# Bias rows written in the first phase, split weights of the output projection kept in DRAM, masks with buffers of their own

## The chip, the core and the metric

The kernel runs on one core of a Trainium2 chip. The metric is device time in microseconds (us) of one execution; lower is better. Engines are named as the profile names them: PE (TensorE matmuls), PEld (its weight loads), DVE (VectorE), ACT (ScalarE), POOL (GpSimd) and SP (SyncE, which here issues every DMA from one queue).

## The reference

One layer for 1024 tokens of width 2048, cut to what matters here:

```python
z = rms_norm(h, norm_g) @ w_in                    # one projection for all branches
o_rw = rwkv7_mixer(z_rw, ...)                     # 16 recurrent heads of 64
# sparse attention, 16 heads, per block of 128 queries:
score = einsum('bqh,bqhs->bqs', wi, relu(einsum('bqhd,bsd->bqhs', qi, k_idx)))
score = where(admissible, score, -inf)            # chunk-causal
_, sel = top_k(score, 256)                        # 256 keys per query
logits = einsum('bqhr,bqkr->bqhk', qa, kv_sel) + bias_tab[t5_bucket(sel - q_pos)]
o_ds = softmax(where(valid, logits, -inf)) @ kv_sel @ w_uv
h = h + concat([o_rw * silu(g_rw), o_ds * silu(g_ds)]) @ w_out
h = h + (p @ w_ple) * sigmoid(h @ w_pg)
out = rms_norm(h, final_g)
```

## The kernel before, in words

Matmuls with weights run on operands split in two fp32r parts (`wh` and `wl`, made by `w_piece`: one 256 KB load, a copy on ACT, a subtraction on POOL), three matmuls for each pair of tiles. A recording layer (`Sched`) takes every instruction with a level and writes out, at each `emit`, an order for all five engines by a list schedule with its own costs; so every instruction has the same line, L382, in the profile, and a small change moves many. An engine runs its instructions strictly in the order written.

The stages are these.

1. Projection and the recurrent branch, in 16 units (8 head pairs by two halves of 512 tokens). At its end PE is filled up with `wout_rw(0)`, the recurrent branch's half of the output projection for the first token half: 16 column tiles `n`, each with two weight pieces `w_o[n, 0]` and `w_o[n, 1]`, 24 matmuls `pz<-mh,wh` and so on. 13 tiles are recorded in this stage, three later.
2. Scoring: for 16 index heads and the query blocks `qt` 2 to 7, PE makes `pix`, ACT `rl` (Relu), DVE adds into the mask row `mk` of that block, `(qt + 1) * 128` wide. PE is filled up with the rest of `wout_rw(0)` and with `wout_rw(1)`, the second token half, which loads and splits the same 32 weight pieces again.
3. Search: the 256th largest score of each row is found bit by bit in 31 rounds, blocks 2 to 4 by counts on DVE (`jk`), blocks 5 to 7 by Sign with a sum on ACT (`js`); DVE turns the counts into the next threshold `th`. Evacuations of `wout_rw(1)` (`h<-pz,h` on DVE, with `h` loaded from `xt`) and the first attention operands stand among it.
4. Masks: `pick_keys(qt)` for `qt` 2 to 7 turns scores and threshold into 0 or -1e30, with two scratch rows `eq` and `gt`.
5. Attention, 8 head pairs `u` by 8 query blocks: `softmax` adds mask and bias (`mb` on POOL, then `lgt` on DVE), takes Exp on ACT; `weigh` transposes and multiplies by the values. Its score rows `lgt` use tag `L` of pool `at`, three buffers of 128x1024; `eq` and `gt` use the same three.
6. The rest of the output projection, the gate and the last norm, where PE sets the time.

The bias rows: 16 heads' bias by distance is a 16x384 table `vb`; `bsk` holds 128 copies of each row in DRAM, so that a skewed read gives a 128x256 tile `bt` for a head. Before the change the table is made between scoring and `wout_rw(1)`, and one DMA writes all 3 MB of `bsk` from SBUF.

The lines that the change and the steps below touch are in `wout_rw`, `pick_keys`, the block under `nc.level(LG)` that starts with `rb0`, and the attention loop over `u` and `qt`.

Of the kernel before, what the change touches and what calls it, by code (L numbers as in the profile page):

```python
# [15 lines left out]
OP = mybir.AluOpType  # L16
# [369 lines left out]
def hybrid_kernel(ctx, tc, cst, msk, bkt, prm, xt, pt_, w_z, w_z80, w_lora, w_uq, w_iq, w_uk, w_uv, w_o, w_pg,  # L386
# [6 lines left out]
    qnd, ckd = ([[dt(f"{n}{j}_{h}", [128, TH]) for h in range(2)] for j in range(m)] for n, m in (("qn", 3), ("ck", 2)))  # L393
    kid = [dt(f"ki{h}", [64, TH]) for h in range(2)]
    gdd, h1d = ([[dt(f"{n}{j}_{h}", [128, TH]) for h in range(2)] for j in range(m)] for n, m in (("gd", 8), ("h1", 16)))
    bsk = dt("bsk", [16, 128, 384])

    def pool(stack, keep=None, **kw):
        p_ = Pool(nc, stack.enter_context(tc.tile_pool(**kw)), kw["bufs"])
# [497 lines left out]
    def wout_in(hf):  # L897
# [9 lines left out]
                nc.gpsimd.tensor_tensor(ML[g][:, k, :], raw, MH[g][:, k, :], op=OP.subtract)  # L907
        return MH, ML

    def wout_rw(hf, MH, ML, tiles):  # L910
        for n in tiles:
            pz = gemm(lambda g: w_o[n, g], 128, 8, lambda k: MH[k // 4][:, k % 4, :], lambda k: ML[k // 4][:, k % 4, :])
            h_ = big_t("h1")
            nc.sync.dma_start(h_, xt[n * 128:n * 128 + 128, hf * TH:hf * TH + TH])
            with nc.level(LEVAC):
                nc.vector.tensor_tensor(h_, pz, h_, op=OP.add)
                store(h1d[n][hf], h_)

    units = [(u, hf) for hf in range(2) for u in range(8)]
    was, Z, RES, Y = {}, {}, {}, {}  # L920
# [24 lines left out]
    with nc.level(LG):  # L945
        Z[0], was[0] = first_unit(0)
        for n, (u, hf) in enumerate(units):
            sub(2 * n)
            if hf == 0:
                with nc.level(LF):  # L950
                    if u < 5:
                        gds(u, hf)
                    elif u == 5:
                        dsa_lat(0)
                if u == 7:
                    for j, pg in zip((5, 6, 7), zgroup((43, 44, 45))):
                        gds(j, 0, pg)
                    sub(2 * n + 1)
                    Z[n + 1], was[1] = first_unit(1)
                    continue  # L960
            elif u == 0:
                with nc.level(LF):
                    dsa_lat(1)
            if n < 15:
                Z[n + 1] = zunit(*units[n + 1])
            sub(2 * n + 1)
        sub(32)
        with nc.level(LF):
            for j in range(8):
                gds(j, 1)  # L970
            MW = wout_in(0)
            wout_rw(0, *MW, range(NWO))
# [67 lines left out]
                                 start=(j == 0), stop=(j == 1))  # L1040
        return pl[:, :Sn]

    def rb(a, i):
        return bass.AP(tensor=a.tensor, offset=a.offset + i * 16, ap=[[0, 32], [1, 16]])

    with nc.level(LX):
        for j in range(3):
            split_in([(0, h, qnd[j][h]) for h in range(2)], QH[:, j, :], QL[:, j, :], nc.vector)
# [25 lines left out]
                        nc.vector.scalar_tensor_tensor(MK[qt], r_, w_, MK[qt], op0=OP.mult, op1=OP.add)  # L1074

    with nc.level(LG):
        rb0 = sm.tile([32, 16], F32, name="rb0")
        nc.sync.dma_start(rb0, rel_bias)
        rb1 = sm.tile([32, 16], F32, name="rb1")
        nc.sync.dma_start(rb1, rb(rel_bias, 15))  # L1080
        nc.vector.tensor_tensor(rb0, rb0, rb1, op=OP.subtract)
        oh = at.tile([32, 384], F32, name="oh", tag="L")
        nc.sync.dma_start(oh, bkt)
        pvb = pg_tile()
        nc.tensor.matmul(pvb[:16, :384], rb0, oh, start=True, stop=True)
        vb = at.tile([16, 384], F32, name="vb", tag="L")
        nc.vector.tensor_copy(vb, pvb[:16, :384])
        nc.sync.dma_start(bsk, vb[:, None, :].to_broadcast([16, 128, 384]))
        MW1 = wout_in(1)
        with nc.level(LF):  # L1090
            wout_rw(0, *MW, range(NWO, 16))
        wout_rw(1, *MW1, range(16))
# [12 lines left out]
    def pick_keys(qt):  # L1105
        Sn = (qt + 1) * 128
        t_, n_ = KEYS[qt][:2]
        eq = at.tile([128, 1024], F32, name="eq", tag="L")[:, :Sn]
        nc.gpsimd.tensor_scalar(eq, MK[qt], t_, None, op0=OP.is_equal)
        gt = at.tile([128, 1024], F32, name="gt", tag="L")[:, :Sn]  # L1110
        nc.vector.tensor_scalar(gt, MK[qt], t_, None, op0=OP.is_gt, op1=OP.add, accum_out=n_)
        nc.vector.tensor_scalar(n_, n_, -1.0, 256.0, op0=OP.mult, op1=OP.add)
        nc.vector.tensor_tensor_scan(MK[qt], one.to_broadcast([128, Sn]), eq, 0.0, op0=OP.mult, op1=OP.add)
        nc.vector.scalar_tensor_tensor(eq, MK[qt], n_, eq, op0=OP.is_le, op1=OP.mult)
        (nc.vector if qt in FINV else nc.gpsimd).tensor_tensor(MK[qt], gt, eq, op=OP.add)
        nc.scalar.activation(MK[qt], MK[qt], AF.Copy, scale=BIG, bias=-BIG)

    def count(qts, sign=False, op=OP.is_ge):
# [13 lines left out]
    with nc.level(LX):  # L1132
        for qt in range(2, 8):
            Sn = (qt + 1) * 128
            nc.vector.memset(MK[qt][0:64, Sn - 64:Sn], NINF)

        for qts in (BY_COUNT, *BY_SIGN):
            th, xm, cn, pd = group(qts)  # L1140
            neg = 0x80000000 if qts in BY_SIGN else 0
            nc.vector.memset(th, 0)
            count(qts)
            nc.vector.tensor_scalar(xm, cn, 255.5, None, op0=OP.is_lt)
            nc.vector.memset(th, 0x40000000 | neg)
            nc.vector.memset(pd, 0xBFFFFFFF ^ neg)
            nc.vector.copy_predicated(th, xm, pd)
        for bit in range(30, -1, -1):
            for qts in (*BY_SIGN, BY_COUNT):
                th, xm, cn, pd = group(qts)  # L1150
                sign = qts in BY_SIGN
                count(qts, sign)
                for qt, x, n, few in ([(qt, *KEYS[qt][2:0:-1], 512.0 - 128 * (qt + 1) - 0.5) for qt in qts] if sign else
                                      [(0, xm, cn, 255.5)]):
                    nc.vector.tensor_scalar(x, n, few, float(1 << bit), op0=OP.is_lt, op1=OP.mult)
                nc.vector.scalar_tensor_tensor(th, xm, (1 << bit) >> 1, th, op0=OP.bitwise_or, op1=OP.bitwise_xor)
        for g, qts in enumerate(BY_SIGN):
            p_, _, cn, _ = group(qts)
            nxt = lambda n, dt: consts.tile([128, len(qts)], dt, name=f"{n}{g}")
            ts, tt = nc.vector.tensor_scalar, nc.vector.tensor_tensor  # L1160
            ts(p_, p_, 0x80000000, None, op0=OP.bitwise_xor)
            lo, hi, sg, up = (nxt(n, U32) for n in ("nlo", "nhi", "nsg", "nup"))
            d, c, b = (nxt(n, F32) for n in ("nd", "nc", "nb"))
            ts(lo, p_, 0xFFFF, None, op0=OP.bitwise_and)
# [12 lines left out]
            ts(sg, cn, 255.5, None, op0=OP.is_ge)
            nc.vector.copy_predicated(p_, sg, up)
        for qt in range(2):
            Sn = (qt + 1) * 128  # L1180
            nc.gpsimd.memset(MK[qt], 0.0)
            nc.gpsimd.memset(MK[qt][0:64, Sn - 64:Sn], -BIG)
        for qt in range(2, NFIN):
            pick_keys(qt)
    CH = xn.tile([128, 2, T], F32R, name="CH", tag="xh0")
    CL = xn.tile([128, 2, T], F32R, name="CL", tag="xl0")
# [124 lines left out]
    with nc.level(LG):  # L1311
# [191 lines left out]
```

## Time and profile before

| what | value |
|---|---|
| median of 3 runs | 2894.11 us (2889.0 to 2895.61) |
| the profiled execution's own time | 2892.14 us |
| its span, first to last instruction | 2890.4 us |
| granted TensorE clock, mean | 0.968 |
| PE busy | 2696.4 us (93%) |
| DVE, ACT, POOL busy | 1641.3, 1500.9, 1381.8 us |
| DMA | 268.15 MB, 93 GB/s over the span |

The profiled execution lies 2.0 us below the median and inside the runs' range. Busy shares are means over stages that have different limits; the stages are told apart by the strips of 40 slices (72 us each) and by windows.

### The profile page before, as it was taken

The numbers are of one execution on the slowest core, as the hardware profiler recorded it, in microseconds if no ns is written. First come the engines' busy times: TensorE is split into PE (matmuls) and PEld (weight loads), VectorE is DVE, ScalarE is ACT, GpSimd is POOL, SyncE is SP. The second block draws the span as 40 slices with busy tenths as digits, with TensorE's granted clock in tenths as the row PEclk, the third lists the DMA queues.
The fourth block names the chain that finished last, engine by engine and source line by source line (L and its number), as shares of the span: only waits on it lengthen the run. The fifth ranks groups of instructions, "written<-read, shape, count | busy, mean of one in ns | idle before, by whom it ended". The sixth has DMA issues, their size and how long they took to land. (4 is left out here: it accounts for less than half of the span.)

```text
span 2890.4 us, 46558 instructions
## 1 busy us (share of the span) xinstructions
PE 2696.4 (93%) x16482; PEld 2158.0 (75%) x16482; DVE 1641.3 (57%) x3709; ACT 1500.9 (52%) x3297; POOL 1381.8 (48%) x1403
## 2 busy tenths in 40 slices
PE   7999999999999999999999999726999999999997
PEld 6777877877787887887877778614776688878885
DVE  5566666446862566666665578777666551125312
ACT  4455555435653455555554566695677533333332
POOL 5544555554464555455445542113333355556564
PEclk9999999999999999999999999858999999999998
DMA  4222222222233222222224533511223243345332
GB/s 156 84 65 61 74 74 76 82 87 70 91 118 91 73 72 67 71 70 70 76 90 152 181 119 106 105 27 27 69 63 93 79 156 95 99 151 172 110 98 91
DMA packets 158489, 268.15 MB, mean 93 GB/s; under 512 B 21648, under 2 KB 43184, under 8 KB 158256
## 3 DMA queue, kind: packets, MB, share of 16 engines
q1 hardware_dynamic: 158256, 265.18, 30.1%
q8 instruction: 130, 2.13, 0.3%
q14 instruction: 103, 0.84, 0.1%
HBM read 221.33 MB, written 35.39 MB: 89 GB/s over the span
## 5 line engine op out<-in xcount | busy, mean ns | idle before, releaser
L382 POOL TENSOR_TENSOR wl<-wr,wh 128x512 fp32r<-128x512 f32 (+2 forms) x656 | 860.2, 1314 | 824.3 <-ACT wh L382 746.8
L382 ACT ACTIVATE wh<-wr 128x512 fp32r<-128x512 f32 (+2 forms) x656 | 403.8, 618 | 752.7 <-PE pz L382 567.5
L382 PE MATMUL pz<-xh,wh 128*128 128x512 f32 (+1 forms) x1504 | 610.1, 408 | 12.8 <-ACT wh L382 9.0
L382 PE MATMUL pz<-xh,wl 128*128 128x512 f32 (+1 forms) x1504 | 610.8, 408 | 1.5 <-POOL wl L382 1.3
L382 PE MATMUL pz<-xl,wh 128*128 128x512 f32 (+1 forms) x1504 | 608.4, 406 | 0.0
L382 PEld LDWEIGHTS pz<-xh,wh 128*128 128x128 f32 (+1 forms) x1504 | 286.1, 190 | 61.6 <-ACT wh L382 10.0
L382 PEld LDWEIGHTS pz<-xh,wl 128*128 128x128 f32 (+1 forms) x1504 | 285.0, 190 | 49.6 <-POOL wl L382 3.0
L382 PEld LDWEIGHTS pz<-xl,wh 128*128 128x128 f32 (+1 forms) x1504 | 285.8, 190 | 47.7 <-DVE xl L382 0.3
L382 DVE SCALAR_TENSOR_TENSOR tg<-tg,pg 128x512 f32<-128x512 f32 x32 | 22.0, 687 | 315.4 <-ACT tg L382 315.4
L382 PE MATMUL pz<-hh,wl 128*128 128x512 f32 x512 | 199.3, 389 | 0.0
L382 PE MATMUL pz<-hh,wh 128*128 128x512 f32 x512 | 199.3, 389 | 0.0
L382 PE MATMUL pz<-hl,wh 128*128 128x512 f32 x512 | 199.2, 389 | 0.0
L382 DVE CAST_PREDICATED QX<-MS,pq 128x512 f16<-128x512 uint8 x160 | 110.2, 689 | 146.9 <-PE pq L382 145.9
L382 POOL TENSOR_TENSOR mb<-mk,bt 128x256 f32<-128x256 f32 (+1 forms) x128 | 90.4, 710 | 161.4 <-DVE mx L382 136.5
L382 ACT ACTIVATE Ztb<-pzt 64x256 f16<-64x256 f32 x320 | 120.6, 377 | 62.4 <-PE pzt L382 57.0
L382 ACT ACTIVATE lgt<-lgt,nm 128x128 f32<-128x128 f32 (+7 forms) x128 | 98.9, 773 | 60.2 <-DVE nm L382 58.8
L382 PEld LDWEIGHTS pz<-hh,wh 128*128 128x128 f32 x512 | 96.1, 188 | 20.0
L382 PEld LDWEIGHTS pz<-hh,wl 128*128 128x128 f32 x512 | 96.1, 188 | 20.0
L382 PEld LDWEIGHTS pz<-hl,wh 128*128 128x128 f32 x512 | 96.1, 188 | 19.9
L382 ACT ACTIVATE js<-mk,th 128x1024 f16<-128x1024 f32 (+2 forms) x93 | 96.7, 1040 | 25.5 <-DVE xm L382 21.4
L382 ACT ACTIVATE Sw<-UV,Wx 64x64 f32<-64x64 f32 x240 | 82.2, 343 | 52.7 <-DVE UV L382 49.4
L382 PE MATMUL pz<-mh,wh 128*128 128x512 f32 x256 | 101.6, 402 | 3.0 <-ACT mh L382 2.3
(331 smaller groups left out, 5981.6 us busy)
## 6 DMA issues: line engine op xcount, KB each, us to landing
wr<-in_w_z_dram SPq DMA_DIRECT2D x368, 256.0 KB, 2.6
wr<-in_w_pg_dram SPq DMA_DIRECT2D x128, 256.0 KB, 2.5
wr<-in_w_o_dram SPq DMA_DIRECT2D x120, 256.0 KB, 2.7
h<-h SPq DMA_DIRECT2D x60, 256.0 KB, 2.7
h<-in_xt_dram SPq DMA_DIRECT2D x32, 256.0 KB, 3.1
out_dram<-h SPq DMA_DIRECT2D x32, 256.0 KB, 2.3
gd<-gd SPq DMA_DIRECT2D x16, 256.0 KB, 2.3
mix<-m SPq DMA_DIRECT2D x32, 128.0 KB, 1.7
```

What stands on the lines that cost most here:

```text
L382: getattr(self.real[o.eng], o.name)(*o.args, **o.kw)
```

## The change

Three edits, and what follows from them.

- **Bias rows.** The table is made in the first unit of stage 1 (`bias_table`), stored to DRAM (`vbd`), and each of the 16 units records one DMA from DRAM to DRAM that writes one head's 128 copies (`bias_copies`). The one DMA of 3 MB between scoring and search is gone, and `oh` and `vb` leave tag `L`.
- **Kept weight parts.** `wout_rw(0)` stores both parts of each of its 32 weight pieces to DRAM (64 stores of 256 KB); `wout_rw(1)` loads both parts (64 loads) instead of loading and splitting the piece again (32 loads, 32 ACT copies, 32 POOL subtractions).
- **Masks.** `gt` is written over the scores in `mk`. `eq` becomes fp16; for blocks 2 to 4 `eq` and the running count `up` use the count's own scratch tag `jk`, for blocks 5 to 7 `eq` uses tag `js` and `up` takes one buffer of tag `L`. Blocks 5, 6 and 7 are recorded inside the attention loop of the first head pair, each one step ahead of the step that needs it (ahead of steps 4, 5 and 6).

```diff
-POOLH, FINV = (), (2, 3, 4, 5, 6, 7)
-NMR, NFIN, FAHEAD, PIECES = 1, 8, 1, (0, 1, 2)
+POOLH = ()
+NMR, PIECES = 1, (0, 1, 2)
...
+    def kept(n, g):
+        if (n, g) in parts:
+            pair = []
+            for d, nm in zip(parts[n, g], ("wh", "wl")):
+                t = wp.tile([128, 4, 128], F32R, name=nm, tag=nm, bufs=W_[1])
+                nc.sync.dma_start(t.bitcast(F32), d)
+                pair.append(t)
+            return pair
+        pair = w_piece(w_o[n, g], 4, 128)
+        parts[n, g] = [dt(f"wo{n}_{g}{a}", [128, 4, 128]) for a in "hl"]
+        for d, t in zip(parts[n, g], pair):
+            nc.sync.dma_start(d, t.bitcast(F32))
+        return pair
...
-            pz = gemm(lambda g: w_o[n, g], 128, 8, ...)
+            pz = pz_tile()
+            for g in range(2):
+                gemm_part(pz, None, 128, 4 * g, 4, 8, ..., kept(n, g))
...
+    def bias_table():
...
+        nc.tensor.matmul(pvb, rb[:, 0], oh, start=True, stop=True)
+        vb = tp.tile([128, TH], F32, name="vbs", tag="zl", bufs=3)[:16, :384]
+        nc.vector.tensor_copy(vb, pvb)
+        nc.sync.dma_start(vbd, vb)
+    def bias_copies(h):
+        nc.sync.dma_start(bsk[h], vbd[h:h + 1].to_broadcast([128, 384]))
...
         for n, (u, hf) in enumerate(units):
             sub(2 * n)
+            with nc.level(LF):
+                if n == 0:
+                    bias_table()
+                bias_copies(n)
...
-        oh = at.tile([32, 384], F32, name="oh", tag="L")
...
-        vb = at.tile([16, 384], F32, name="vb", tag="L")
-        nc.vector.tensor_copy(vb, pvb[:16, :384])
-        nc.sync.dma_start(bsk, vb[:, None, :].to_broadcast([16, 128, 384]))
...
-        eq = at.tile([128, 1024], F32, name="eq", tag="L")[:, :Sn]
+        small = lambda n: at.tile([128, 640], F16, name=n, tag="jk", bufs=2)
+        eq = (small("eq") if qt in BY_COUNT else at.tile([128, 1024], F16, name="eq", tag="js", bufs=1))[:, :Sn]
+        up = (small("up") if qt in BY_COUNT else at.tile([128, 1024], F32, name="up", tag="L"))[:, :Sn]
         nc.gpsimd.tensor_scalar(eq, MK[qt], t_, None, op0=OP.is_equal)
-        gt = at.tile([128, 1024], F32, name="gt", tag="L")[:, :Sn]
-        nc.vector.tensor_scalar(gt, MK[qt], t_, None, op0=OP.is_gt, op1=OP.add, accum_out=n_)
+        nc.vector.tensor_scalar(MK[qt], MK[qt], t_, None, op0=OP.is_gt, op1=OP.add, accum_out=n_)
         nc.vector.tensor_scalar(n_, n_, -1.0, 256.0, op0=OP.mult, op1=OP.add)
-        nc.vector.tensor_tensor_scan(MK[qt], one.to_broadcast([128, Sn]), eq, 0.0, op0=OP.mult, op1=OP.add)
-        nc.vector.scalar_tensor_tensor(eq, MK[qt], n_, eq, op0=OP.is_le, op1=OP.mult)
-        (nc.vector if qt in FINV else nc.gpsimd).tensor_tensor(MK[qt], gt, eq, op=OP.add)
+        nc.vector.tensor_tensor_scan(up, one.to_broadcast([128, Sn]), eq, 0.0, op0=OP.mult, op1=OP.add)
+        nc.vector.scalar_tensor_tensor(eq, up, n_, eq, op0=OP.is_le, op1=OP.mult)
+        nc.vector.tensor_tensor(MK[qt], MK[qt], eq, op=OP.add)
...
-        for qt in range(2, NFIN):
+        for qt in BY_COUNT:
             pick_keys(qt)
...
-                for q in range(NFIN, 8):
-                    if u == 0 and (q - FAHEAD == qt or q - FAHEAD < qt == 0):
-                        pick_keys(q)
+                if u == 0 and qt + 1 not in BY_COUNT and 1 < qt < 7:
+                    pick_keys(qt + 1)
```

How the written order moves, at three places. First DVE behind the last threshold of the search (`th` of blocks 5 and 6). Before the change, where `mk_18657` and `mk_18658` are the rows of blocks 5 and 6:

```order
L382 COPY_PREDICATED th_19085<-nsg_19291,nup_19292 128x2
L382 TENSOR_SCALAR gt,cn_19088<-mk_18657,th_19085 128x768
L382 TENSOR_SCALAR cn_19088<-cn_19088 128x1
L382 SCALAR_TENSOR_TENSOR mk_18657<-one,eq 128x768
L382 SCALAR_TENSOR_TENSOR eq<-mk_18657,cn_19088,eq 128x768
L382 TENSOR_TENSOR mk_18657<-gt,eq 128x768
L382 TENSOR_SCALAR gt,cn_19088<-mk_18658,th_19085 128x896
L382 SCALAR_TENSOR_TENSOR mk_18658<-one,eq 128x896
```

and with the change, where `mk_18814`, `mk_18815` and `mk_18816` are the rows of blocks 4, 5 and 6:

```order
L382 COPY_PREDICATED th_19218<-nsg_19424,nup_19425 128x2
L382 ISA lgt,mx<-plg,mb,mx 128x128
L382 ISA mx 128x1
L382 TENSOR_TENSOR mt<-po_21579,gr_21585 128x128
L382 ISA lgt,mx<-plg,mb,mx 128x128
L382 ISA mx 128x1
L382 ISA lgt,mx<-plg,mk_18814 128x384
L382 ISA mx 128x1
L382 TENSOR_SCALAR nm<-mx 128x1
L382 SCALAR_TENSOR_TENSOR qs_21615<-pg,qs_21615 64x512
L382 ISA lgt,mx<-plg,mb,mx 128x128
L382 ISA mx 128x1
```

Attention step 4 of the first head pair now stands right behind the threshold; steps 0 to 3 stand among the search, and the masks 5, 6 and 7 come one by one between steps 4, 5, 6 and 7.

Second, SP where scoring's operands (`lraw`, `rq`) are loaded. Before the change:

```order
L382 DMA wr<-in_w_o_dram 128x512
L382 DMA h_0_153<-h_3962 128x512
L382 DMA wr<-in_w_o_dram 128x512 x2
L382 DMA lraw<-qn_0_107 128x512
L382 DMA lraw<-qn_1_108 128x512
```

and with the change:

```order
L382 DMA wo_0h<-wh 128x512
L382 DMA h_0_153<-h_4007 128x512
L382 DMA wo_0l<-wl 128x512
L382 DMA wo_1h<-wh 128x512
L382 DMA h_4043<-in_xt_dram 128x512
L382 DMA wo_1l<-wl 128x512
L382 DMA mix_3_90<-m 128x256
L382 DMA wr<-in_w_o_dram 128x512 x2
L382 DMA h_0_155<-h_4019 128x512
L382 DMA wr<-in_w_o_dram 128x512 x2
L382 DMA lraw<-qn_0_107 128x512
L382 DMA lraw<-qn_1_108 128x512
```

Stores of kept parts now stand between the weight loads, ahead of scoring's operands.

Third, SP in stage 1, behind the second load of `upr`, with the change:

```order
L382 DMA upr<-in_w_lora_dram 128x256
L382 DMA wr<-in_w_z_dram 128x512 x3
L382 DMA vb<-vbs 16x384
L382 DMA wr<-in_w_z_dram 128x512
L382 DMA bsk<-vb 128x384 x10
L382 DMA wr<-in_w_z_dram 128x512
L382 DMA bsk<-vb 128x384 x6
L382 DMA wr<-in_w_z_dram 128x512 x5
```

The 16 copies of bias rows are issued as a burst in the second unit, among the weight loads, and not one in each unit. Over the whole of PE's order, 311 matmuls of `wout_rw` stood ahead of scoring's first `pix` and 302 more up to its last; now 344 and 238.

## Rows read from the trace of the kernel before

**Rows 1.** Page, part 2: busy tenths and granted clock in 40 slices.
```profile
PE   7999999999999999999999999726999999999997
PEclk9999999999999999999999999858999999999998
DMA  4222222222233222222224533511223243345332
```
**Rows 2.** Windows: stretch, length, busy us (instructions) of PE, PEld, DVE, ACT, POOL, PEclk, DMA share, GB/s.
```profile
1600.00:1790.00 190.00, 186.66 (x848) 151.67 (x846) 138.91 (x152) 122.92 (x184) 75.00 (x57) 1.00 0.41 133
1790.00:1823.00 33.00, 33.00 (x145) 27.14 (x145) 25.66 (x93) 18.59 (x33) 10.04 (x8) 1.00 0.71 129
1878.00:1976.00 98.00, 17.91 (x48) 12.12 (x48) 79.00 (x289) 76.21 (x137) 18.65 (x11) 0.55 0.09 22
1960.40:1979.70 19.30, 1.27 (x3) 0.68 (x3) 17.69 (x24) 2.29 (x4) 10.77 (x4) 0.56 0.02 7
```
**Rows 3.** Timeline of SP, DVE, ACT in the search: start, us, engine, instruction [idle before <-releaser].
```profile
1803.55 0.66 SPq L382 DMA_DIRECT2D bsk<-vb  x1
1804.31 8.07 SPq L382 DMA_DIRECT2D h<-in_xt_dram  x1
...
1837.28 0.69 DVE L382 TENSOR_TENSOR h<-pz,h 128x512 f32<-128x512 f32 x1 [19.35 <-DMA h<-in_xt_dram]
...
1838.14 1.04 ACT L382 ACTIVATE js<-mk,th 128x896 f16<-128x896 f32 x1 [21.02 <-DVE xm L382]
```
**Rows 4.** DMA issues by line: count, KB each, median us from issue to landing.
```profile
bsk<-vb SPq DMA_DIRECT2D x1, 3072.0 KB, 33.0
...
bt<-bsk SPq DMA_DIRECT2D x16, 128.0 KB, 2.1
```
**Rows 5.** Groups on ACT, 1799 to 1960: count | busy us, mean ns | idle before.
```profile
L382 ACT ACTIVATE js<-mk,th 128x1024 f16<-128x1024 f32 x31 | 35.6, 1148 | 1.7 <-DVE js L382 0.9
...
L382 ACT ACTIVATE wh<-wr 128x512 fp32r<-128x512 f32 x4 | 2.5, 624 | 0.0
```
**Rows 6.** Groups on ACT and DVE in attention's first steps, 1976 to 2012.
```profile
L382 ACT ACTIVATE lgt<-lgt,nm 128x256 f32<-128x256 f32 x2 | 1.0, 499 | 0.0
L382 ACT ACTIVATION_READ_ACCUMULATOR lgt<-lgt,nm 128x1 f32 x15 | 2.8, 190 | 0.0
...
L382 DVE CUSTOM_DVE_ANT_0 lgt<-plg,mk 128x512 f32<-128x512 f32 x6 | 4.1, 684 | 1.8 <-PE ptt L382 1.8
L382 DVE CUSTOM_DVE_ANT_0 lgt<-plg,mb,mx 128x256 f32<-128x256 f32 x9 | 4.3, 480 | 0.4
```
**Rows 7.** Timeline of DVE and PE: last threshold, attention's restart, second head pair's first row.
```profile
1960.29 0.16 DVE L382 COPY_PREDICATED th<-nsg,nup 128x2 uint32<-128x2 uint32 x1
...
1976.89 0.58 PE L382 MATMUL plg<-kh,qs 128*128 128x256 f32 x1 [17.91 <-DVE mx L382]
...
2011.04 0.28 DVE L382 CUSTOM_DVE_ANT_0 lgt<-plg,mb 128x128 f32<-128x128 f32 x1
```
**Rows 8.** Groups on POOL and DVE in scoring, 1600 to 1790.
```profile
L382 POOL TENSOR_TENSOR wl<-wr,wh 128x512 fp32r<-128x512 f32 x33 | 48.2, 1464 | 79.2 <-ACT wh L382 55.3 <-ACT rl L382 8.6 <-PE pix L382 8.0
...
L382 DVE SCALAR_TENSOR_TENSOR mk<-rl,WI,mk 128x896 f32<-128x896 f32 x15 | 21.7, 1449 | 1.7 <-ACT rl L382 1.7
L382 DVE SCALAR_TENSOR_TENSOR mk<-rl,WI,mk 128x1024 f32<-128x1024 f32 x15 | 21.2, 1415 | 0.6 <-ACT rl L382 0.6
```
**Rows 9.** Windows of 10 us where scoring's operands are loaded (columns as in rows 2).
```profile
1590.00:1600.00 10.00, 10.00 (x47) 8.16 (x46) 2.75 (x11) 2.53 (x4) 5.12 (x5) 1.00 0.44 133
1600.00:1610.00 10.00, 10.00 (x46) 8.29 (x45) 1.92 (x2) 3.61 (x5) 4.67 (x8) 1.00 0.93 323
1610.00:1620.00 10.00, 9.08 (x39) 6.85 (x38) 7.18 (x7) 6.65 (x11) 8.19 (x6) 1.00 0.95 293
```
**Rows 10.** Timeline of SP and ACT in stage 1: weight loads and a later split.
```profile
175.52 7.88 SPq L382 DMA_DIRECT2D wr<-in_w_z_dram  x5
...
198.03 0.63 ACT L382 ACTIVATE wh<-wr 128x512 fp32r<-128x512 f32 x1
```

More of the change, by code (lines that the diff above doesn't have):

```diff
@@ L395, in hybrid_kernel @@
     gdd, h1d = ([[dt(f"{n}{j}_{h}", [128, TH]) for h in range(2)] for j in range(m)] for n, m in (("gd", 8), ("h1", 16)))
-    bsk = dt("bsk", [16, 128, 384])
+    bsk, vbd = dt("bsk", [16, 128, 384]), dt("vb", [16, 384])
+    parts = {}
     def pool(stack, keep=None, **kw):
@@ L908, in wout_in @@
         return MH, ML
+    def kept(n, g):
[11 more added lines that the diff above has]
+        return pair
     def wout_rw(hf, MH, ML, tiles):
         for n in tiles:
-            pz = gemm(lambda g: w_o[n, g], 128, 8, lambda k: MH[k // 4][:, k % 4, :], lambda k: ML[k // 4][:, k % 4, :])
+            pz = pz_tile()
+            for g in range(2):
+                gemm_part(pz, None, 128, 4 * g, 4, 8, lambda k: MH[k // 4][:, k % 4, :], lambda k: ML[k // 4][:, k % 4, :],
+                          kept(n, g))
             h_ = big_t("h1")
@@ L917, in wout_rw @@
                 store(h1d[n][hf], h_)
+    def bias_table():
+        rb = sm.tile([32, 2, 16], F32, name="rb", bufs=1)
+        for i in range(2):
+            nc.sync.dma_start(rb[:, i], bass.AP(tensor=rel_bias.tensor, offset=rel_bias.offset + i * 15 * 16,
+                                                ap=[[16 - 16 * i, 32], [1, 16]]))
+        nc.vector.tensor_tensor(rb[:, 0], rb[:, 0], rb[:, 1], op=OP.subtract)
+        oh = tp.tile([128, TH], F32, name="oh", tag="zl", bufs=3)[:32, :384]
+        nc.sync.dma_start(oh, bkt)
+        pvb = ps.tile([128, TH], F32, name="pvb", tag="pi", bufs=3)[:16, :384]
+        nc.tensor.matmul(pvb, rb[:, 0], oh, start=True, stop=True)
[4 more added lines that the diff above has]
+        nc.sync.dma_start(bsk[h], vbd[h:h + 1].to_broadcast([128, 384]))
     units = [(u, hf) for hf in range(2) for u in range(8)]
@@ L1041, in score @@
         return pl[:, :Sn]
-    def rb(a, i):
-        return bass.AP(tensor=a.tensor, offset=a.offset + i * 16, ap=[[0, 32], [1, 16]])
     with nc.level(LX):
@@ L1076, in hybrid_kernel @@
     with nc.level(LG):
[L1077 to L1081, printed above, removed]
-        oh = at.tile([32, 384], F32, name="oh", tag="L")
-        nc.sync.dma_start(oh, bkt)
-        pvb = pg_tile()
-        nc.tensor.matmul(pvb[:16, :384], rb0, oh, start=True, stop=True)
-        vb = at.tile([16, 384], F32, name="vb", tag="L")
-        nc.vector.tensor_copy(vb, pvb[:16, :384])
-        nc.sync.dma_start(bsk, vb[:, None, :].to_broadcast([16, 128, 384]))
         MW1 = wout_in(1)
```

## The prediction

> **What bounds the kernel now.** I read the strips of 40 slices first. PE stands at nine tenths in all but a few slices; the hole is in slices 26 to 28 of 72 us, 1806 to 2023 us, where PE falls to 7, 2 and 6 tenths and the granted clock to 8, 5, 8 [rows 1]. So the time is PE's, except from about 1800 to 2000 us, where something else sets it. The windows say what: scoring is PE's (186.66 of 190 us), the second half of the search is not (17.91 of 98), and in the 19.3 us of the last masks DVE works 17.69 and PE 1.27 [rows 2]. Clock costs nothing there: PE runs at 0.55, the 1.2 GHz level, but mostly waits.
>
> The timeline comes next. At 1803.55 SP issues the 3 MB `bsk` DMA, and behind it at 1804.31 an `h` load. DVE stands 19.35 us for that `h`, until 1837.28, and ACT, whose counts wait for DVE, 21.02 us until 1838.14 [rows 3]. The DMA view gives 33.0 us from issue to landing for `bsk` [rows 4]: 1803.55 + 33.0 = 1836.6, just before DVE goes on. Outside this hole the search is ACT's chain of `js`: the widest form ran 31 times at 1148 ns with only 1.7 us of idle time ahead of it [rows 5]. Last, after the final threshold at 1960.29 PE first works again for attention at 1976.89, after 17.91 us of nothing, and the second head pair's first DVE row starts at 2011.04 [rows 7], 50.8 us behind the threshold.
>
> **The sum.** It is made against the profiled execution's own 2892.1 us, 2.0 below the median.
>
> *1. The big DMA leaves the search: -19.4 us.* The whole DVE stall of [rows 3] is on the path, since ACT stands through it. Ends: -21.0 if ACT's idle time counts whole. At the other end the written order has eight `h` evacuations among the search instead of six; if the two added ones each cost their 0.69 us [rows 3] and a wait of 2.1 us, the nearest load [rows 4], 5.6 us is given back: -13.8. I take the stall as measured, because a lone load has the engines to itself.
>
> *2. Attention steps 0 to 3 stand among the search: +2 us.* ACT's chain takes in five Exp of 128 to 384 columns, at about 0.5 us with 0.19 us for the sum [rows 6], 3.4 us, two copies (1.0 at the same duration) and one evacuation of a mask row (1.1, at most a `js` of 1148 ns). It loses four `wh` at 0.624 [rows 5], 2.5 us, and one evacuation of `qs` (about 0.6). Net 2.4, of which the 1.7 us of idle time in [rows 5] hide a little. Ends: 0 if the steps fit into waits, +5.5 if the removed `wh` lay beside other work.
>
> *3. Masks 5 to 7 between the steps: -9 us.* From the last threshold to the second pair's first row DVE took 50.8 us. With the change it still has the mask work, 17.7 us [rows 2], and eight score rows of steps 4 to 7, some 1.8 us each (two wide parts at 684 ns, a biased one at 480 ns [rows 6]), 14.5 us. To that I add 5 us of evacuations and 5 us of waits, an estimate of seven hand-overs at the 0.7 us of one wide part: 42 us. PE's 17.91 us of nothing should be broken up, not vanish. Ends: -17 if neither waits nor evacuations show; +3 if each of the three masks makes its step wait for a new hand-over of about 1 us and nothing else is gained. What is late next is DVE, which does masks and score rows alone.
>
> *4. Kept parts in scoring and its surroundings: -3 us.* In the written order 31 matmuls of `wout_rw` fewer stand up to scoring's last `pix` (344 + 238 against 311 + 302). One costs 33.00/145 = 0.228 us [rows 2], so PE's part ends 7.1 us sooner; they aren't lost but moved into the search, where PE has room. The 32 `wl` of 1464 ns on POOL and 32 `wh` on ACT vanish and save nothing by themselves in scoring: PE hides them, and DVE and POOL have time over there (138.91 and 75.00 of 190 [rows 2]; the longest DVE rows show 1.7 us of idle time or less in 21.7 [rows 8], so DVE runs through only in their stretch). Against this stands traffic: a column tile of `wout_rw(0)` now moves two pieces in, four parts out, and an `xt` load and an `h` store, eight times 256 KB = 2.1 MB, while its 24 matmuls last 5.5 us. The fastest window moved 323 GB/s at a DMA share of 0.93, another 293 at 0.95 [rows 9]; so a tile needs 6.5 to 7.2 us, 1.0 to 1.7 more than PE gives it, 13 to 22 us over 13 tiles if PE waits for all of it. PE waits for loads only, and just before that stretch the share is 0.44 at 133 GB/s [rows 9]; a third of 13 is lost, I take it, +4. Ends: -10 (the 3.3 us in which PE wasn't busy go too) and +15.
>
> The Trainium skill speaks of this too: "DMA: Bandwidth & Descriptors", section Bandwidth, has a lone core's large load at 425 GB/s, bound by its engines, and smaller transfers well below. By that figure, as an estimate, a tile's bytes would take 4.9 us, the +4 would go and the sum would end at 2861. The windows above, with the engines busy, show 323 at most, and I go by them.
>
> In `wout_rw(1)` loads double from 32 to 64. The search's DMA share is 0.09 in its second half [rows 2], which hides them; without that cover each further 256 KB would cost some 0.8 us at 323 GB/s.
>
> *5. Sixteen bias copies in the first phase: +2 us.* They go out as one burst among the weight loads of the second unit: 16 issues at about 0.66 us [rows 3], and 3.1 MB. That takes 9.7 us at 323 GB/s, 33 as the one DMA did [rows 4], or 52 at the 2.1 us of each 128 KB [rows 4]. The loads issued from 175.52 to 183.4 feed splits up to 198.03 and beyond [rows 10], so 15 to 20 us lie between a load and its use. At 9.7 nothing is lost; at 33 some 13 to 18. I take +2, nearer to the fast end, since weight loads are interleaved and PE has pieces in hand. Ends: 0, for nothing is taken away there, and +15. Bias table, its small store and the extra buffers for masks: nothing, they lie beside 1600 us of PE work at nine tenths [rows 1].
>
> -19.4 + 2 - 9 - 3 + 2 = -27.4, so **2865 us**.
>
> **Rivals.**
>
> *A. Traffic of the kept parts binds.* Scoring's operands `lraw` stand in SP's order behind the stores, and the first ten microseconds of those loads already ran at 0.93 to 0.95 of the engines [rows 9]. Term 4 goes to +15: 2865 + 18 = 2883, with 2878 to 2895 around it. For it: no other stretch of the kernel is that near the limit. Against: the strip of DMA reads 4 and 5 tenths there, not 9 [rows 1].
>
> *B. Slower: SP becomes the chain.* Stores of a piece must wait in SP's order for POOL's `wl`, and the next weight loads stand behind them. If this ends the prefetch, a piece costs 2.1 us of load, 0.62 of `wh`, 1.46 of `wl` and two issues at 0.66, together 5.5 us, against 2.74 us of its 12 matmuls. With seven of 26 pieces in hand, 19 x 2.76 = 52 us are lost, term 4 becomes -7 + 52 = +45, and the time 2865 + 48 = 2913. It decides as soon as a piece's turn on SP is longer than 2.74 us with no buffer in hand. For it: SP is in order. Against: POOL's 79.2 us of idle time ahead of `wl` are mostly waits for ACT's `wh` (55.3) [rows 8], so POOL has time to stay ahead.
>
> *C. A new wait takes the old one's place.* DVE's eight evacuations in the search need kept parts, two loads where one was. If each waits one load's 2.1 us [rows 4], 17 us come back: 2882. For it: DVE is in order and thresholds stand behind `h`. Against: DMA is nearly idle there.
>
> *D. The change doesn't take the stall away*, because the `h` load itself is slow: it occupied SP for 8.07 us [rows 3]. Then term 1 is 0: 2884. Against: it landed right behind `bsk`.
>
> *E. More than forecast.* Terms 3 and 4 at their good ends: 2865 - 8 - 7 = 2850 or less.
>
> **How the numbers follow.** A measurement of this kernel can tell about 0.2% from no change, 5.8 us: below 2886.3 is faster, above 2897.9 slower. Forecast (2850 to 2878) 0.62; E 0.09, all faster; A 0.13, of it 0.09 faster and 0.04 the same; C 0.06, 0.05 and 0.01; D 0.03, 0.02 and 0.01; B 0.07, slower. Faster 0.87, same 0.06, slower 0.07. The range from 2843 to 2886 leaves out B (0.07), the upper parts of A, C and D (0.06) and the last of E (0.05), 0.18 together.
>
> **What the changed profile would show.** Term 1: no DVE idle time of some 19 us ahead of an `h` in the search; if one over 5 us stands there, C or D holds. Term 2: `js` still 31 of a kind with little idle time, and Exp of 128 to 384 columns among them. Term 3: under 45 us from the last `th` to the second pair's first row; masks 5 to 7 between score rows. Term 4: scoring's last `pix` some 3 us earlier against the first phase's end; PE at nine tenths from 1500 to 1620; DMA there well above 133 GB/s. PE idle time behind `wh`, `wl` or `lraw` of more than 10 us is A, of over 40 is B. Term 5: no PE or ACT wait for `wr` from 170 to 240 us. A forecast that fails in sign must fail in term 4 or 5, the only ones that reach +15.

## The result, and the profile after

| | before | with the change |
|---|---|---|
| median of 4 runs each, us | 2892.26 | 2846.89 |
| ratio, 95% interval | | 0.9844 [0.9827, 0.9861] |
| profiled execution: own time, span | 2892.14, 2890.4 | 2844.57, 2842.8 |
| PE, ACT, POOL busy, us | 2696.4, 1500.9, 1381.8 | 2701.8, 1482.0, 1336.5 |
| DMA, MB | 268.15 | 293.36 |

45 us less by the medians; 27.4 had been forecast, and 2846.9 lies just inside the range (2843 to 2886). So the sign and the places were right, and the size was too small. The two profiled executions differ by 47.6 us. The readings below divide them at the same marks: the first matmul of `wout_rw` (its weight load), scoring's first and last `pix`, the first `js` (on DVE), the last `th`, the second head pair's first score row.

| us from mark to mark | before | after | difference | early bias alone | masks ahead |
|---|---|---|---|---|---|
| start to first `wout_rw` matmul | 1511.9 | 1512.5 | +0.6 | 1515.9 | 1513.1 |
| to first `pix` | 106.5 | 115.9 | +9.4 | 107.0 | 116.6 |
| to last `pix` (scoring) | 167.8 | 148.6 | -19.3 | 166.9 | 148.3 |
| to first `js` | 6.4 | 5.3 | -1.0 | 7.4 | 5.3 |
| to last `th` (search) | 167.7 | 144.7 | -23.0 | 146.2 | 142.7 |
| to second pair's first row | 50.8 | 37.2 | -13.5 | 51.2 | 56.5 |
| to last score row | 285.6 | 284.9 | -0.6 | 286.2 | 285.8 |
| to the end | 593.8 | 593.6 | -0.1 | 593.6 | 593.3 |

The last two columns are experiments below. In the strips of the page after, PE's hole [rows 1] has shrunk from three slices to two, its clock stands at 6 and 8 tenths there, and DMA reads 7 and 8 tenths in the two slices from 1492 us on.

```profile
PE   7999999999999999999999999948999999999996
PEclk9999999999999999999999999968999999999998
DMA  4232222232332222222227844511223343355332
```

The windows by the same marks (first `wout_rw` matmul, first `pix`, last `pix`, last `th`, second pair), with the columns of [rows 2]: first the two up to scoring's end before, then the four after. PE is busy in scoring nearly without a gap, with 72 fewer instructions than before (684 against 756); the stretch ahead of it moves 284 GB/s at a DMA share of 0.84.

```profile
1512.00:1618.40 106.40, 98.49 (x579) 78.96 (x575) 51.41 (x106) 47.95 (x113) 57.58 (x51) 0.95 0.53 171
1618.40:1786.20 167.80, 165.38 (x756) 135.38 (x757) 127.64 (x142) 112.19 (x169) 60.95 (x44) 1.00 0.35 116
...
1512.50:1628.40 115.90, 109.28 (x620) 87.67 (x619) 61.35 (x109) 49.26 (x115) 57.77 (x52) 0.96 0.84 284
1628.40:1776.90 148.50, 147.96 (x684) 121.97 (x683) 116.87 (x136) 96.39 (x144) 27.28 (x19) 1.00 0.45 150
1776.90:1927.10 150.20, 104.20 (x527) 82.86 (x526) 136.46 (x558) 133.95 (x252) 21.41 (x25) 0.80 0.32 100
1927.10:1964.20 37.10, 25.43 (x147) 18.34 (x149) 29.67 (x79) 17.24 (x32) 16.06 (x14) 0.77 0.04 13
```

What ACT waited for in the search, first before (1786 to 1960 us), then after (1777 to 1927). The columns are the sum in us, how often, and the longest.

```profile
ACT js L382 <- DVE xm L382: 21.4, 2, 21.0
ACT wh L382 <- PE pz L382: 8.5, 4, 3.1
ACT hk L382 <- issue: 3.5, 1, 3.5
```

```profile
ACT js L382 <- DVE js L382: 8.0, 1, 8.0
ACT js L382 <- DVE xm L382: 1.5, 3, 1.0
ACT PT L382 <- PE ptt L382: 1.1, 2, 0.8
```

The stall of 21.0 us is gone. So are ACT's waits ahead of `wh` copies, 8.5 us; but ACT's chain did not wait for them. All four lie ahead of ACT's first count at 1799.64 us, and what released that count was DVE, which makes the first counts of blocks 5 to 7 itself. After, one wait of 8.0 us for the same counts of DVE stands in their place. The end of that start before, on ACT and DVE:

```profile
1798.11 0.63 ACT L382 ACTIVATE wh<-wr 128x512 fp32r<-128x512 f32 x1 [2.09 <-PE pz L382]
1798.60 1.00 DVE L382 TENSOR_SCALAR_CACHE_REDUCE js<-mk,th 128x768 f16<-128x768 f32 x1
1799.64 1.15 ACT L382 ACTIVATE js<-mk,th 128x1024 f16<-128x1024 f32 x1 [0.90 <-DVE js L382]
```

So the search is told better in two parts, split at ACT's first count; the last three columns are experiments below.

| us | before | after | early bias alone | masks ahead | no kept parts |
|---|---|---|---|---|---|
| first `js` on DVE to ACT's first | 7.05 | 4.18 | 5.03 | 4.18 | 5.04 |
| from there to the last `th` | 160.65 | 140.55 | 141.21 | 138.55 | 145.55 |

DVE's timeline after, at the last threshold: a score row of step 4 follows at once. The second pair's first row comes 37.2 us after the threshold, against 50.8 [rows 7].

```profile
1926.98 0.15 DVE L382 COPY_PREDICATED th<-nsg,nup 128x2 uint32<-128x2 uint32 x1
1927.05 0.34 DVE L382 CUSTOM_DVE_ANT_0 lgt<-plg,mb,mx 128x128 f32<-128x128 f32 x1
...
1964.21 0.28 DVE L382 CUSTOM_DVE_ANT_0 lgt<-plg,mb 128x128 f32<-128x128 f32 x1
```

The 16 bias copies of the first phase, in the DMA view, where one DMA took 33.0 us [rows 4]:

```profile
bsk<-vb SPq DMA_DIRECT2D x16, 192.0 KB, 5.4
```

### The profile page after: what moved, and what is told of

It is laid out like the page before. It is cut to its first block, busy times and chain, and to the rows that moved or that the text cites. A ratio compares the mean times of both kernels' runs of the same rounds, so it can differ in the third digit from the quotient of the medians.

```text
span 2842.8 us, 46633 instructions
## 1 busy us (share of the span) xinstructions
PE 2701.8 (95%) x16482; PEld 2157.9 (76%) x16482; DVE 1644.8 (58%) x3709; ACT 1482.0 (52%) x3265; POOL 1336.5 (47%) x1371
## 2 busy tenths in 40 slices
DMA packets 172586, 293.36 MB, mean 103 GB/s; under 512 B 23440, under 2 KB 44992, under 8 KB 172352
## 5 line engine op out<-in xcount | busy, mean ns | idle before, releaser
L382 POOL TENSOR_TENSOR wl<-wr,wh 128x512 fp32r<-128x512 f32 (+1 forms) x624 | 812.8, 1306 | 773.5 <-ACT wh L382 720.4
L382 ACT ACTIVATE wh<-wr 128x512 fp32r<-128x512 f32 (+1 forms) x624 | 384.1, 617 | 731.7 <-PE pz L382 536.1
L382 PE MATMUL pz<-xh,wh 128*128 128x512 f32 (+1 forms) x1504 | 609.5, 407 | 11.5 <-ACT wh L382 7.6
L382 PEld LDWEIGHTS pz<-xh,wh 128*128 128x128 f32 (+1 forms) x1504 | 285.6, 190 | 62.5 <-ACT wh L382 9.4
L382 PEld LDWEIGHTS pz<-xl,wh 128*128 128x128 f32 (+1 forms) x1504 | 285.8, 190 | 45.9 <-DVE xl L382 0.3
L382 PE MATMUL ptt<-C,lgt 128*128 128x128 f32 x576 | 99.7, 289 | 23.8 <-ACT lgt L382 22.4
L382 PE MATMUL po<-PT,V 128*64 128x128 f32 x1152 | 87.6, 287 | 18.7 <-ACT PT L382 18.2
```

The lines of the kernel that those rows point to most:

```text
L382: getattr(self.real[o.eng], o.name)(*o.args, **o.kw)
```

## The experiments

The first five runs each undo an edit or a part of one, or make one edit alone; the others ask what bounds the stretches of the kept parts. All ratios are against the kernel before, run on the same chip beside them. "Fill" is what the plan puts into PE's gaps: matmuls of `wout_rw`.

**Late bias rows.**

```diff
...
-                bias_copies(n)
...
+        vb = at.tile([16, 384], F32, name="vb", tag="L")
+        nc.vector.tensor_copy(vb, pvb[:16, :384])
+        nc.sync.dma_start(bsk, vb[:, None, :].to_broadcast([16, 128, 384]))
```

> The changed kernel with the bias table and its one 3 MB DMA back between scoring and search. Theory 'stretches add': the three edits act on stretches of their own, and only ACT's stall in the search (21 us) comes back: 2847 + 21 = 2868, ratio to the kernel before 0.992; the last threshold to the second head pair stays near 37 us. Rival 'the early rows carry the mask edit too': steps 0 to 3 need the bias tile, stand in order behind the DMA, and hold DVE longer or lose their place, so 21 + 13 = 34 us come back: 2881, ratio 0.996. Rival 'the h load itself is slow': without the DMA the stall was gone for another reason, under 5 us come back: 2850.

Measured: 2872.64 us, 0.9921 [0.9907, 0.9934]. The search is 168.5 us long, 23.7 more than with the change, and the mask stretch stays at 36.5. The stretches add, as the theory had it; the mask edit doesn't need early rows. The waits of this kernel in the search show what stood behind the DMA (33.4 us here): an `h` load as before, and a kept part as well.

```profile
ACT js L382 <- DVE th L382: 25.5, 5, 21.4
...
PE pz L382 <- DMA wh<-wo_0h: 22.0, 1, 22.0
DVE h L382 <- DMA h<-in_xt_dram: 21.2, 1, 21.2
```

**Early bias rows alone**, on the kernel before.

```diff
+                bias_copies(n)
...
-        nc.sync.dma_start(bsk, vb[:, None, :].to_broadcast([16, 128, 384]))
```

> The kernel before with the early bias rows alone. Theory 'stretches add': ACT's stall of 21.0 us goes, nothing else: 2892 - 21 = 2871, ratio 0.9927. Rival 'half is taken by the next wait': wh copies waiting for PE and the h loads take some of it, -10: 2882, ratio 0.9965. Rival 'the edit gives more than its stall': -26, 2866, ratio 0.991.

Measured: 2876.25 us, 0.9930 [0.9918, 0.9943], 20 us. The search loses 21.5 us (167.7 to 146.2) and every other stretch stays within 1.1 us, but for the first, 3.9 longer in this one execution; with the change, and with the copies in it, that stretch is only 0.6 longer. Of the 21.5 us, 19.4 lie behind ACT's first count and 2.0 ahead of it. ACT still waits 7.6 us for PE ahead of `wh`, again before its first count.

**No kept parts.**

```diff
         pair = w_piece(w_o[n, g], 4, 128)
-        parts[n, g] = [dt(f"wo{n}_{g}{a}", [128, 4, 128]) for a in "hl"]
-        for d, t in zip(parts[n, g], pair):
-            nc.sync.dma_start(d, t.bitcast(F32))
         return pair
```

> The changed kernel with wout_rw(1) loading and splitting its weight pieces again, nothing stored. Theory: last pix comes back by 9.8 us less the first phase's share, and in the search ACT waits again behind its wh copies for PE (8.5 us in the kernel before): +10 +5 = 2862, ratio 0.990. Rival 'only PE's moved matmuls count': +7, 2854, ratio 0.987. Rival 'traffic of the stores had cost something': +3 or less, 2850, ratio 0.985.

Measured: 2865.95 us, 0.9898 [0.9885, 0.9912]: as the theory had it, the kept parts are worth 15.6 us beside the other two edits. The first `pix` comes 8.4 us earlier (107.5), scoring is 18.1 longer (166.7), the search 5.9 longer (150.6), the mask stretch 2.3 longer.

**Masks ahead of attention**, in the new buffers.

```diff
-        for qt in BY_COUNT:
+        for qt in range(2, 8):
             pick_keys(qt)
...
-                if u == 0 and qt + 1 not in BY_COUNT and 1 < qt < 7:
-                    pick_keys(qt + 1)
```

> The changed kernel with masks 5, 6 and 7 recorded ahead of attention, in the new buffers. In the written order no score row stands ahead of the last threshold then. Theory: last threshold to second head pair goes back from 37 to 50.7 us, +13.5, and the search loses its five Exp, copies and 13 score rows, -5: 2847 + 8.5 = 2855, ratio 0.987. Rival 'buffers do it, not the place': no change, 2847, ratio 0.9844. Rival 'ACT had room for the steps': +13.5, 2860, ratio 0.989.

Measured: 2864.48 us, 0.9894 [0.9878, 0.9909]. The search is 2.0 us shorter without the attention steps in it, and 56.5 instead of 37.2 us follow, more than any of its three forecasts had, and nearly 6 more than in the kernel before. In that stretch PE waits 45.9 us for DVE's rows.

```profile
PE plg L382 <- DVE mx L382: 45.9, 5, 32.5
```

**Old buffers, masks between the steps.**

```diff
...
-        eq = (small("eq") if qt in BY_COUNT else at.tile([128, 1024], F16, name="eq", tag="js", bufs=1))[:, :Sn]
-        up = (small("up") if qt in BY_COUNT else at.tile([128, 1024], F32, name="up", tag="L"))[:, :Sn]
+        eq = at.tile([128, 1024], F32, name="eq", tag="L")[:, :Sn]
+        up = MK[qt]
+        gt = at.tile([128, 1024], F32, name="gt", tag="L")[:, :Sn]
...
```

> The changed kernel with the masks' old buffers (eq and gt of 128x1024 in tag L, the running count over the scores), still between the steps. In the written order six score rows stand ahead of the last threshold instead of 13, and no Exp in the search. Theory 'place and buffers both': the search is 2 us shorter, as in the run with masks ahead (142.7), but from the last threshold to the second head pair some 45 to 50 us pass instead of 37.2: 2847 - 2 + 10 = 2855, ratio 0.987. Rival 'the place alone does it': 2847, 0.9844. Rival 'the buffers alone do it': as with masks ahead, 2864, 0.9894.

Measured: 2863.92 us, 0.9894 [0.9878, 0.9911]; mask stretch 51.0 us, search 144.2. The time is the second rival's, but its reason isn't. With the old buffers the place between the steps gains nothing against the 50.8 of before; with the new ones the place ahead of attention loses 6. Only both together give 37.2. What the buffers cost shows in DVE's wait for transposes that still read score rows of tag `L`:

```profile
DVE gt L382 <- PE ptt L382: 7.5, 3, 3.6
```

**Every part stored twice**, 16.8 MB more.

```diff
+        for a, t in zip("hl", pair):
+            nc.sync.dma_start(dt(f"wx{n}_{g}{a}", [128, 4, 128]), t.bitcast(F32))
```

> The changed kernel with both parts of each weight piece of wout_rw(0) stored twice, 16.8 MB more. In the changed kernel the stretch from the first wout_rw matmul to the first pix lasts 115.9 us at 284 GB/s and a DMA share of 0.84. Theory 'PE waits for loads only and the stores have slack of 16 per cent': with 16.8 MB more (435 GB/s wanted) the slack is used up; at 330 GB/s the stretch would need some 150 us, of which stores behind the last load cost nothing, so first pix comes 15 to 35 us later and the time is 2862 to 2882, ratio 0.990 to 0.997. Rival 'stores never hold PE': 2849, ratio 0.985. Rival 'SP's order, not bytes, is what binds': the 64 further issues at about 0.7 us cost 45 us, 2892, ratio 1.0.

Measured: 2866.87 us, 0.9901 [0.9887, 0.9916], some 16 us slower than the change. The stretch up to the first `pix` lasts 11.5 us longer, and 6.8 us more stand ahead of its first `wout_rw` matmul in this execution. The time lies at the theory's lower end, and both rivals fall; the stretch itself grew by less than the theory's 15. Its window from that matmul to the first `pix` shows the engines full, and PE stopping (112.33 of 127.4):

```profile
1519.30:1646.70 127.40, 112.33 (x592) 88.12 (x593) 55.90 (x103) 47.63 (x109) 58.53 (x53) 0.89 0.98 346
```

In the middle of it 40 us went at 389 GB/s (a packet counts in the window in which it starts, so a share can pass 1):

```profile
1561.00:1601.00 40.00, 39.23 (x242) 31.10 (x241) 18.98 (x39) 16.80 (x48) 17.84 (x15) 1.00 1.05 389
```

So with single stores, at 284 GB/s, there is room.

**Only `wl` kept.**

```diff
+            nc.scalar.activation(wh, wr, AF.Copy)
...
-        for d, t in zip(parts[n, g], pair):
-            nc.sync.dma_start(d, t.bitcast(F32))
+        nc.sync.dma_start(parts[n, g], pair[1].bitcast(F32))
```

> The changed kernel in which only wl of each piece is stored and loaded again; wh is copied on ACT from the weight load as before the change. Stores halve to 8.4 MB. Theory 'fill sets scoring above a floor of 148 us': 252 fill matmuls in scoring against 238, 14 x 0.228 = 3.2 us, so scoring lasts 151 to 152 us though 24 wh copies stand on ACT; first pix comes 3 to 5 us earlier (fewer stores ahead of lraw, 335 fills against 344); in the search seven wh copies wait for PE again, +3 to +6. Together 2847 + 3 - 4 + 4 = 2850, ratio 0.9855. Rival 'ACT's wh copies set scoring': scoring lasts 160 us or more, 2860, ratio 0.989.

Measured: 2857.62 us, 0.9872 [0.9856, 0.9889]. First `pix` 3.2 us earlier, search 4.6 longer (149.3), as expected; scoring 155.6, 4 more than the first theory and 4 less than the rival. That part stays between the two; PE's busy time there rose by 4.9 us and its granted clock is 0.99. Keeping `wh` as well gains some 8 us by the two ratios, though its stores cost 3.2 ahead of the first `pix`.

**Eleven tiles in the first phase.**

```diff
-NRL, LHP, NWO = 3, 3, 13
+NRL, LHP, NWO = 3, 3, 11
```

> The changed kernel with 11 instead of 13 tiles of wout_rw(0) recorded in the first phase: 312 fill matmuls ahead of the first pix instead of 344, and two tiles' 2 MB of stores fewer ahead of scoring's operands. Theory 'stores stand ahead of the operands in SP's order': first pix comes 5 to 7 us earlier (32 x 0.228 = 7.3); scoring with 258 instead of 238 fills is 4.6 us longer; 2847 - 6 + 4.6 = 2846, ratio 0.984. Rival 'fills weren't what the first pix waits for': first pix stays, 2852, ratio 0.986.

Measured: 2856.2 us, 0.9867 [0.9851, 0.9883]. A miss. The first `pix` comes 4.7 us earlier, just short of the theory's 5 to 7, but scoring lasts 11.8 longer (160.3) for 20 more fill matmuls in the order, 4.6 us. PE's busy time there rose by 7.0 us, at a granted clock of 0.99 against 1.00, and its idle time by 4.8. The rest isn't settled; PE waits there for a kept part's load, 1.6 us, as it doesn't with the change.

**Fill held back from scoring.** The plan may not put matmuls of `wout_rw(1)` ahead of scoring's last `pix`: all 16 tiles (K is 0), or the last 12 (K is 4).

```diff
...
-        wout_rw(1, *MW1, range(16))
+        wout_rw(1, *MW1, range(K))
+        nc.gate = LASTPIX
+        wout_rw(1, *MW1, range(K, 16))
...
```

> The changed kernel with all matmuls of wout_rw(1) held back in the plan until scoring's last pix: 40 instead of 238 fill matmuls in scoring, 384 instead of 186 behind it. PE is busy 147.96 of 148.5 us in scoring, DVE 116.9. Theory 'PE is the only bound of scoring': it shortens by up to 45 us, held at DVE's 117 plus its waits, so by some 25; in the search PE has 46 us free, but attention's score matmuls need the PSUM of wout_rw, so the first steps come after the last threshold again (+19 as with masks ahead): 2847 - 25 + 19 = 2841, ratio 0.9825. Rival 'scoring is bound by the latency of its own chain': 10 or less is saved, 2856, ratio 0.988.

> The same, but only the last 12 tiles of wout_rw(1) are held back: 136 fill matmuls in scoring, 288 behind it, and steps 0 to 3 still in the search by the written order. Theory 'PE is the only bound of scoring': 102 matmuls at 0.228 us leave it, 23 us, and go into the search's 46 us of free PE time; 2847 - 18 to - 23 = 2827, ratio 0.977. Rival 'latency of scoring's own chain': saves 5 to 10, 2840, ratio 0.982. Rival 'the steps of the first head pair are late': last threshold waits or steps move behind it, +15: 2842, ratio 0.983.

Measured: 2853.78 us, 0.9856 [0.9841, 0.9872] for all, 2849.97, 0.9856 [0.9830, 0.9881] for 12. Scoring stayed at 148.3 and 150.0 us with 40 and 136 fill matmuls. By the ratios the first lies between its theory and its rival, the second above all three that were expected. That PE is the only bound of scoring is refuted (with 40 it is busy 115.4 of 148.3 us): there is a second floor, right below the change. PE's waits in scoring with 12 held back:

```profile
PE pix L388 <- DVE qs L388: 12.9, 8, 2.4
PE pg L388 <- DVE qs L388: 2.5, 4, 1.0
PE pix L388 <- ACT rl L388: 0.6, 2, 0.4
```

**The next heads' `qs` first.** In scoring, the evacuations that make `qs` had the rank of fill, behind every `rl` and `mk`. Here they rank ahead, with 12 and with all 16 tiles held back.

```diff
-            list(qstacks(w_iq[u, 0], "q", 1.0, qs, LHP))
+            list(qstacks(w_iq[u, 0], "q", 1.0, qs, LEVAC))
```

> The kernel with 12 tiles held back to scoring's end, and scoring's evacuations of qs ranked ahead of rl and mk in the plan instead of behind them; the same 136 fill matmuls in scoring. There, PE waited longest for DVE's qs, and DVE for ACT's qs. Theory 'the floor of 148 us is the late evacuation of the next heads' qs': scoring falls to between 125 and 135 us, the search takes 0 to 3 us more, 2850 - 18 = 2832, ratio 0.979. Rival 'the floor is ACT's and DVE's rl and mk': scoring stays at 148 to 150, 2849, ratio 0.985. Rival 'moved evacuations stall rl': slower, 2858, ratio 0.988.

Measured: 2835.61 us, 0.9792 [0.9778, 0.9807]: faster than both kernels. Scoring lasts 135.1 us, PE's wait ahead of `pix` for `qs` is 1.4 us instead of 12.9, and the search (145.4) and mask stretch (37.9) stay. The floor was the late `qs`, and what it did to the clock: with the same 582 PE instructions PE's busy time fell from 133.7 to 128.3 us as its granted clock rose from 0.97 to 1.00, and its idle time by some 10.

```profile
PE pix L388 <- ACT rl L388: 2.9, 5, 0.8
PE pg L388 <- DVE qs L388: 2.0, 3, 0.9
PE pix L388 <- DVE qs L388: 1.4, 2, 0.9
```

> As the run with scoring's qs evacuations ranked first, but all 16 tiles of wout_rw(1) held back to scoring's end: 40 instead of 136 fill matmuls in scoring. Theory 'in scoring PE is the bound again (128 of 135 us) and DVE the next (117.6)': scoring falls from 135 to 120 to 126 us; search and mask stretch together stay near 183 us, as they did between 16 and 12 tiles held back without the rank (183.1 and 183.8): 2835.6 - 12 = 2824, ratio 0.975. Rival 'DVE and ACT chain is the floor at 135': 2836, ratio 0.979. Rival 'the fill now pushes attention's first steps behind the search': +8 behind the last threshold and nothing back in the search, 2832, ratio 0.978.

Measured: 2844.61 us, 0.9829 [0.9813, 0.9845], a miss: scoring went up to 142.7 us, and the search and mask stretch came to 183.6 as expected. With less fill, PE stops more and its clock falls. Two windows of 10 us of scoring with all tiles held back:

```profile
1661.00:1671.00 10.00, 7.65 (x34) 5.67 (x33) 8.26 (x10) 6.09 (x11) 3.04 (x3) 0.99 0.43 118
1671.00:1681.00 10.00, 8.05 (x23) 6.33 (x23) 5.05 (x5) 7.32 (x11) 5.62 (x3) 0.67 0.51 167
```

The mean granted clock over these 142.7 us is 0.92; with 12 tiles held back and `qs` first each such window has 1.00.

## Why the prediction came out as it did

**Term 1, -19.4.** Right, to the figure. From ACT's first count on, early bias alone took 19.4 us (160.65 to 141.21), as long as DVE's stall; in the changed kernel, taking it back cost 24.3. Rivals C and D fell: DVE's `h` waits for no DMA any more.

**Term 2, +2; measured -0.7.** From ACT's first count on, the search lasts 141.21 us with early bias alone and 140.55 with the change. The attention steps cost 2.0 of it (138.55 with masks ahead), where the sum had 4.9 without the `wh` copies. The removal of these the sum priced by their busy time, 2.5 us, and that was sound: kept parts and new buffers together gave 2.7; with the old buffers it was 1.1 (140.07). Without kept parts the changed kernel takes 5.0 us more there. ACT's idle time has 4.6 of it, among which 1.9 us ahead of `qs` copies for PE and 2.2 more ahead of `js` for DVE; its busy time is nearly the same, as fewer of the steps stand in the search. So there more than the copies' own time comes back, and why is not shown.

What no term had is the start, -2.9. Before, a wait of 1.70 us for PE and a predicated copy of 1.24 us stood among DVE's first counts. With early bias alone the wait is gone and the copy takes 1.00; with the change it takes 0.15.

**Term 3, -9; measured -13.5.** Mechanism right, a size off. I had 17.7 us of masks, 14.5 of score rows, 10 of evacuations and waits. In the window after, DVE's score rows sum to 9.7 us, by the groups; masks come to some 16.5, and 10.8 are left for evacuations and waits. Three of these groups:

```profile
L382 DVE CUSTOM_DVE_ANT_0 lgt<-plg,mk 128x512 f32<-128x512 f32 x6 | 4.1, 684 | 0.1
L382 DVE CUSTOM_DVE_ANT_0 lgt<-plg,mb,mx 128x256 f32<-128x256 f32 x5 | 2.4, 481 | 0.3
...
L382 DVE TENSOR_TENSOR_SCAN up<-one,eq 128x1024 f32<-128x1024 f32 x1 | 2.3, 2270 | 0.0
```

The step that failed is "eight score rows of steps 4 to 7, some 1.8 us each". The price of a part, 684 and 480 ns [rows 6], was right, but no row has two parts of 512: the widest, step 7's, is one of 512 and two of 256. Step 4's rows are narrower still, and one of its parts stood ahead of the threshold.

**Term 4, -3; measured -10.9** (first `pix` +9.4, scoring -19.3, first `js` -1.0). Up to the last `pix`, PE's busy time fell by 6.6 us (98.5 + 165.4 to 109.3 + 148.0), against 7.1 forecast from the order. The step that failed is "a third of 13 is lost, I take it, +4": PE's idle time did not rise by 4 but fell by 3.2, from 10.4 to 7.2. The bytes came about as estimated: by rate and length the stretch moved 14.7 MB more than before, and 52 stores of 256 KB are 13.6. But 323 GB/s was no limit: the trace of the kernel before already has 393 from 8 to 18 us, at a DMA share of 1.05, and stores doubled ran at 389 for 40 us. At that rate a tile's 2.1 MB take 5.4 us, no more than its matmuls, so there was nothing to lose. Rival A's bound is reached only with stores doubled. Rival B didn't happen either: PE is busy 109.28 of 115.9 where the stores stand.

The reading "scoring is PE's" was true of the kernel before but with a margin that the profile hid: fill made PE look bound down to 148 us, where the late `qs` take over. The change's 238 fill matmuls bring PE just down to it. Why PE lost its last waits isn't shown. DVE's `mk` rows of 128x896 got faster as POOL's `wl` left (1449 to 1146 ns), but those of 128x512 got slower (788 to 889), and with `wl` kept alone they were fast too (1185) while scoring lasted 155.6.

**Term 5, +2; measured +0.6**, or nothing that one execution can show: early bias alone had +3.9 there. The burst took 16.2 us from its first issue at 155.1 to its last landing, between the 9.7 and the 33 of the sum (the 52 should read 50, 24 times 2.1; nothing rests on it). Its sign, no wait for `wr` from 170 to 240 us, was no good test: ACT waited 2.4 us there, and 2.6 in the kernel before. PE was busy 38.04 of the 40 us from 165, against 36.54 before.

So rival E, "more than forecast", held, at a chance of 0.09, through terms 3 and 4 and a start of the search that the sum didn't have. Of the 20 us by which the profiled execution beat the forecast, term 4 has 7.9 and term 3 has 4.5. The sum's ends were wide enough, its middle leaned to caution twice on one side: traffic was priced where nothing waited, and score rows as wider than they are. The errors have one sign and none cancelled another; that the time still lies inside the range, by 4 us, is owed to the width of the ends and not to the sum.

## What to carry to other kernels

An idle time ahead of an operation isn't what the operation costs: ask first what released the next link of the chain. Four `wh` copies showed 8.5 us of waits, but ACT's chain began only when DVE's counts were done, and with no attention steps in the search, taking the copies away gave 1.1 to 2.7 us, about their own time. A rate read from one busy window isn't the limit of the engines: look for the fastest window of the whole trace before pricing traffic by it. An engine that is full because a plan pours filler into its gaps isn't shown to be the bound: ask what the stretch would last without the filler, and take out some of it to see. Two edits that free buffers and move the work they held can each be worth nothing or less alone, and so belong in one forecast.

## What the runs showed of the hardware

With filler taken out of scoring, PE's granted clock fell below 1.00 of 2.4 GHz in windows of 10 us where PE had been stopping for `qs`: with all tiles held back to 0.50, the 1.2 GHz level, behind a window in which PE was busy 5.76 us; with `qs` first as well to 0.67, behind one with 7.65. In the latter run scoring had 96 matmuls fewer than with 12 tiles held back and lasted 7.6 us longer. Filler paid for itself there. With `qs` first and 12 tiles held back, PE's busy time for the same 582 instructions was 128.3 us at a mean of 1.00, against 133.7 at 0.97 without the rank.

Two such windows, all tiles held back without the rank (columns as in [rows 2]):

```profile
1662.00:1672.00 10.00, 5.76 (x20) 3.61 (x19) 10.00 (x8) 5.77 (x9) 6.75 (x4) 0.85 0.25 79
1672.00:1682.00 10.00, 6.47 (x16) 4.48 (x15) 6.33 (x8) 4.77 (x7) 2.99 (x2) 0.50 0.10 29
```

The DMA engines, at a share of 0.98, moved 346 GB/s over 127 us of mostly 256 KB transfers (stores doubled), 389 over 40 us of it; with the change the fastest 10 us (from 1610) moved 398, against 323 in the rows that the prediction went by. The figure of 425 GB/s for one large load, from the Trainium skill ("DMA: Bandwidth & Descriptors", section Bandwidth), was reached by no window of 10 us here; but the estimate that the prediction drew from it, that term 4's +4 would go, came nearer to what was measured than the one from 323.
